# A transformer block's prelude: one modulation sum on VectorE, one on TensorE, and x normed in place

## The chip, the cores and the metric

The kernel runs on one core of a Trainium2 chip. TensorE multiplies matrices, VectorE and ScalarE work element by element, GpSimd does a few copies and subtractions, and SyncE (SP) issues nearly all transfers. The metric is device time in microseconds. Smaller is better.

## The reference, cut to what matters

One block for a sequence of 1024 tokens of width 1024 in float32: an adaptive modulation from a vector c, a token mixer of two branches (an attention with a forget gate and a recurrent one), and a convolutional feed-forward part. The prelude is its first lines:

```python
mod = jax.nn.silu(c) @ w_mod[l] + b_mod[l]
shift1, scale1, gate1, shift2, scale2, gate2 = jnp.split(mod, N_MOD, axis=-1)
u = modulate(rms_norm(h, ln1_g[l]), shift1, scale1)   # xn * (1 + scale) + shift
proj = u @ w_in
```

`w_mod` is 1024 x 6144. The prelude needs the two of its six segments that give shift1 and scale1, each 1024 x 1024 (eight tiles of 128 rows, 512 KB a tile). x is eight such tiles too. u is wanted with the model dimension on the partitions, so x is transposed on the way.

## The kernel before, in words

**Tiling.** Partitions are 128 wide. u is held as two tiles of 128 x 8 x 1024: `u_hi`, a copy rounded to the type fp32r, and `u_lo`, what the rounding left. A product with a weight is three matmul passes (hi x hi, hi x lo, lo x hi), and each weight tile `raw_in` is split in the same way by a ScalarE cast (`hi_in`) and a VectorE subtraction (`lo_in`).

**The prelude** (the block that opens the pools `st` and `stp`) has its own order on SP, VectorE, ScalarE and TensorE: written order.

- `load_x` issues the eight x tiles in two halves of four; each takes a slot of the tag `xt` (eight slots).
- `square` sums the squares of each x tile on ScalarE, and `norm_x` makes the reciprocal root for a half, `rstd`, and four scaled identity matrices `dg` from it.
- `warm(n)` issues n matmuls of 128 x 384 whose results nobody reads (tile `idle`).
- `turn` transposes a 128-column piece of a half by four matmuls against `dg`, so that norm and transpose are one; ScalarE copies the result from PSUM (two slots of tag `tp`) into `uf`. Sixteen turns, half 0 first. A float32 matmul is two instructions in the profile, so the 64 products are 128 records.
- `mod_load` issues the eight weight tiles of a segment: of scale first (four slots of tag `mw`), then of shift (slots of `xt` and `mw` by turns, as they come free).
- `mod_add` multiplies a weight tile with one element of silu(c) for each partition and adds it to `acc`, on VectorE; `mod_sum` then sums `acc` over the partitions with eight matmuls against a column of ones (tile `mps`). First scale is done (giving `A1`), then shift (giving `m1`), with warm matmuls between.
- Two weight tiles of `w_in` (`low_raw`: 24 and 25), `w2`, `g2` and the rest of the constants are loaded behind.
- `u_steps` makes u column by column: VectorE scales and shifts `uf` in place, ScalarE rounds it to `u_hi`, VectorE subtracts to `u_lo`. `low_part` follows each column with four matmuls (tile `low`), and with sixteen more when a half is complete. Between columns 3 and 4, and 5 and 6, of half 0 VectorE also splits the two `w_in` tiles.

**Behind the prelude**, `weave` mixes the products of the other `w_in` tiles (`rkv_items`: tile `ps_rkv`) with the decay chains. TensorE's order is written by the same walk in the program; those of the other engines come from a scheduler. `load_w` brings a `w_in` tile through one of two slots of tag `raw`, which `low_raw` and `w2` use too; the first of them is issued while u is still being made.

Of the kernel before, what the change touches and what calls it, by code (L numbers as in the profile page):

```python
# [9 lines left out]
F32 = mybir.dt.float32  # L10
F32R = mybir.dt.float32r
AF = mybir.ActivationFunctionType
ALU = mybir.AluOpType
# [118 lines left out]
def hybrid_block(ctx: ExitStack, tc: tile.TileContext, a, out):  # L132
# [122 lines left out]
    def load_w(src, name, pool=None, n=1024, scale=None, tags=("whi", "wlo"), bufs=2):  # L255
# [14 lines left out]
        else:  # L270
            nc.scalar.copy(hi, raw)  # L271
# [73 lines left out]
    with ExitStack() as es:  # L345
# [67 lines left out]
        with tc.tile_pool(name="st", bufs=1) as st, tc.tile_pool(name="stp", bufs=2, space=PS) as stp, \  # L413
# [17 lines left out]
            def norm_x(half):  # L431

                hs = slice(half * 4, half * 4 + 4)
                rms_rstd(rstd[:, hs], ssq[:, hs])
                for j in range(half * 4, half * 4 + 4):
                    ts(dg[:, j, :], ident, rstd[:, j : j + 1], None, op0=ALU.mult)

            def mod_load(i, tags):
                ws = [st.tile([128, D], F32, tag=tags[kt % len(tags)], name=f"wm{i}{kt}", bufs={"mw": 4, "xt": 8}[tags[kt % len(tags)]])
                      for kt in range(KT)]  # L440
                for kt, w in enumerate(ws):
                    nc.sync.dma_start(w, a["w_mod"][kt * 128 : kt * 128 + 128, i * D : i * D + D])
                return ws, st.tile([128, D], F32, name=f"acc{i}")
# [6 lines left out]
            def mod_add(kt, ws, acc):  # L450
                if kt == 0:
                    ts(acc, ws[kt], sc[:, 0:1], None, op0=ALU.mult)
                else:
                    stt(acc, ws[kt], sc[:, kt : kt + 1], acc, op0=ALU.mult, op1=ALU.add)

            def mod_sum(i, acc):
                for j0 in (0, 4):
                    ps = stp.tile([128, 4], F32, tag="mp", name=f"mps{i}{j0}")
                    for j in range(4):
                        c0 = (j0 + j) * 128  # L460
                        mm(ps[:, j : j + 1], acc[:, c0 : c0 + 128], ones[:, 0:1], start=True, stop=True)
                    tt(m1[:, i * 8 + j0 : i * 8 + j0 + 4], ps, V("b_mod", i * 8 + j0, 4), op=ALU.add)
                    if i == 1:
                        stt(A1[:, j0 : j0 + 4], m1[:, 8 + j0 : 12 + j0], 1.0, V("ln1_g", j0, 4), op0=ALU.add, op1=ALU.mult)

            def turn(kt, half, xs):
                ps = stp.tile([128, NH], F32, tag="tp", name=f"tr{half}_{kt}")
                for j in range(4):
                    mm(ps[:, j * 128 : j * 128 + 128], xs[j][:, kt * 128 : kt * 128 + 128], dg[:, half * 4 + j, :], start=True, stop=True)
                return ps  # L470

            def u_steps(half):

                cs = slice(half * NH, half * NH + NH)
                for kt in range(KT + 1):
                    if kt < KT:
                        x = uf[half][:, kt, :]
                        ts(x, x, A1[:, kt : kt + 1], m1[:, kt : kt + 1], op0=ALU.mult, op1=ALU.add)
                        nc.scalar.copy(u_hi[:, kt, cs], x)
# [30 lines left out]
            dg = xwa.rearrange("p (j s) -> p j s", s=128)  # L510
            idle = pb.tile([128, NH], F32, tag="big", name="idle")
            xs = [load_x(half) for half in range(2)]
            m = [mod_load(1, ("mw",)), None]
            uf = [st.tile([128, KT, NH], F32, name=f"uf{half}") for half in range(2)]
            warm(28)
# [3 lines left out]
            for half in range(2):  # L519
                for kt in range(KT):  # L520
                    nc.scalar.copy(uf[half][:, kt, :], turn(kt, half, xs[half]))
            m[1] = mod_load(0, ("xt", "mw"))
# [8 lines left out]
            for i in (1, 0):  # L531
                for kt in range(KT):
                    mod_add(kt, *m[1 - i])
                mod_sum(i, m[1 - i][1])
                warm((6, 40)[i])
# [1436 lines left out]
```

## Time and profile before

| | |
|---|---|
| median of 3 runs | 1701.49 us (1699.32 to 1701.51) |
| the profiled execution: its time | 1699.35 us |
| its span, first to last instruction | 1697.6 us |
| mean granted TensorE clock over the span | 0.991 |
| busy: TensorE, VectorE, ScalarE, GpSimd | 97%, 72%, 48%, 8% |
| first transpose of the prelude | 12.88 us |
| VectorE's first addition of a weight tile | 17.46 us |
| first column of u (VectorE, L478) | 47.16 us |
| first matmul behind the low products (`ps_rkv`) | 75.08 us |

All starts in the text are microseconds from the first instruction. Each engine works off its own queue in order; a busy share says how long it worked, not whether anyone waited for it. "PEclk" in the windows is the share of TensorE's full clock that was granted. The matmul records overlap, and their ends are modelled, so a rate is read from how many start in a stretch, not from the length of one.

### The profile page before, as it was taken

The numbers are of one execution on the slowest core, as the hardware profiler recorded it, in microseconds if no ns is written. First come the engines' busy times: TensorE is split into PE (matmuls) and PEld (weight loads), VectorE is DVE, ScalarE is ACT, GpSimd is POOL, SyncE is SP. The second block draws the span as 40 slices with busy tenths as digits, with TensorE's granted clock in tenths as the row PEclk, the third lists the DMA queues.
The fourth block names the chain that finished last, engine by engine and source line by source line (L and its number), as shares of the span: only waits on it lengthen the run. The fifth ranks groups of instructions, "written<-read, shape, count | busy, mean of one in ns | idle before, by whom it ended". The sixth has DMA issues, their size and how long they took to land.

```text
span 1697.6 us, 26285 instructions
## 1 busy us (share of the span) xinstructions
PE 1649.3 (97%) x9886; PEld 1351.7 (80%) x9886; DVE 1218.1 (72%) x2402; ACT 810.7 (48%) x1482; POOL 127.8 (8%) x151
## 2 busy tenths in 40 slices
PE   7999999999999998999989999999999999999998
PEld 7767877787877777888878888888888888888886
DVE  4776787778776624888767534897777777787677
ACT  5553334334354555766732223654444444454455
POOL 0010101111111001212022000000000000000000
PEclk9999999999999999999999999999999999999999
DMA  8487743533332226543177611133332233484463
GB/s 329 145 310 207 194 129 93 137 104 113 99 114 79 93 70 163 145 125 109 39 291 267 223 62 63 50 106 103 121 106 100 93 118 106 158 290 149 128 215 109
DMA packets 120975, 239.87 MB, mean 141 GB/s; under 512 B 39888, under 2 KB 48336, under 8 KB 120848
## 3 DMA queue, kind: packets, MB, share of 16 engines
q1 hardware_dynamic: 112896, 220.94, 39.5%
q0 software_dynamic: 7952, 17.25, 3.8%
q8 instruction: 78, 1.28, 0.3%
q14 instruction: 49, 0.40, 0.1%
HBM read 172.59 MB, written 65.54 MB: 140 GB/s over the span
## 4 chain that ended last, share of the span: by engine, by line
PE 82%; DVE 9%; DMA 4%; ACT 3%; issue 1%; SPq 1%; DVEq 0%; ACTq 0%
PE X L140 13%; PE D L140 12%; PE Y L140 6%; PE gt L140 6%; PE wo L140 5%; PE br L140 5%; PE ps_rkv L140 5%; PE qk L140 4%; PE W L140 3%; PE rk_ps L140 3%; PE v L140 2%; PE ov L140 2%; PE lg L140 2%; PE sp L140 2%; PE tr L140 2%; PE tp L144 2%
## 5 line engine op out<-in xcount | busy, mean ns | idle before, releaser
L140 PE MATMUL D<-op,op 128*128 128x512 f32 x924 | 209.8, 389 | 0.0
L140 PEld LDWEIGHTS D<-op,op 128*128 128x128 f32 x924 | 173.4, 188 | 36.3 <-DVE op L1235 0.3
L140 PE MATMUL X<-T_m,S 128*128 128x512 f32 x440 | 107.2, 390 | 0.2
L140 PEld LDWEIGHTS X<-T_m,S 128*128 128x128 f32 x440 | 82.5, 188 | 18.2 <-ACT x L1511 0.6
L1234 ACT CAST op<-g 128x512 fp32r<-128x512 f32 x77 | 47.8, 621 | 73.4 <-PE D L140 48.3
L1235 DVE TENSOR_TENSOR op<-g,op 128x512 fp32r<-128x512 f32 x77 | 53.0, 688 | 41.3 <-ACT op L1234 41.2
L1471 DVE SCALAR_TENSOR_TENSOR c<-ab,vec,c 128x512 f32<-128x512 f32 x88 | 65.9, 750 | 19.5 <-ACT c L1474 17.9
L779 DVE TENSOR_TENSOR t<-E,M 128x60 f32<-128x60 f32 (+24 forms) x248 | 57.2, 231 | 31.5 <-DMA M<-sm 26.2
L273 DVE TENSOR_TENSOR lo_in<-raw_in,hi_in 128x512 fp32r<-128x512 f32 x84 | 56.4, 706 | 30.0 <-PE gt L140 12.1
L1435 DVE TENSOR_TENSOR S<-ur,S 128x512 fp32r<-128x512 f32 x66 | 45.5, 691 | 35.4 <-ACT S L1431 35.2
L1431 ACT CAST S<-ur 128x512 fp32r<-128x512 f32 x66 | 41.0, 622 | 55.6 <-DVE ur L1424 30.6
L1435 DVE TENSOR_TENSOR A<-ur,A 128x512 fp32r<-128x512 f32 x64 | 44.0, 688 | 31.2 <-ACT A L1431 31.0
L271 ACT CAST hi_in<-raw_in 128x1024 fp32r<-128x1024 f32 x42 | 43.9, 1048 | 46.9 <-PE ps_rkv L140 16.9
L140 PE MATMUL Y<-T_h,A 128*128 128x512 f32 x264 | 63.4, 389 | 0.0
L140 PE MATMUL Y<-T_h,S 128*128 128x512 f32 x264 | 63.3, 389 | 0.0
L1051 ACT ACTIVATE P<-lg,nm 128x896 f32<-128x896 f32 (+3 forms) x64 | 47.5, 743 | 28.6 <-DVE nm L1047 19.6
L140 PE MATMUL X<-B_b,A 128*128 128x512 f32 x252 | 60.8, 390 | 0.0
L140 PE MATMUL W<-B_f,A 128*128 128x512 f32 x252 | 60.6, 389 | 0.0
L781 DVE TENSOR_TENSOR E<-E,t 128x60 f32<-128x60 f32 (+24 forms) x248 | 53.7, 216 | 5.8
L140 PEld LDWEIGHTS Y<-T_h,A 128*128 128x128 f32 x264 | 49.6, 188 | 10.3
L140 PEld LDWEIGHTS Y<-T_h,S 128*128 128x128 f32 x264 | 49.6, 188 | 10.3
L1431 ACT CAST A<-ur 128x512 fp32r<-128x512 f32 x64 | 39.9, 623 | 34.5 <-PE X L140 31.5
(469 smaller groups left out, 4163.9 us busy)
## 6 DMA issues: line engine op xcount, KB each, us to landing
raw_in<-in_w_in SPq DMA_DIRECT2D x50, 512.0 KB, 4.1
wm<-in_w_mod SPq DMA_DIRECT2D x48, 512.0 KB, 6.7
ur<-in_w_up SPq DMA_DIRECT2D x44, 512.0 KB, 4.1
g<-d_g SPq DMA_DIRECT2D x35, 512.0 KB, 3.7
d_g<-gs SPq DMA_DIRECT2D x44, 256.0 KB, 2.0
d_g<-c SPq DMA_DIRECT2D x33, 256.0 KB, 4.5
d_st<-qh SPq DMA_DIRECT2D x64, 128.0 KB, 2.5
d_gate<-gs SPq DMA_DIRECT2D x32, 256.0 KB, 3.0
```

Source lines behind the costliest of these rows:

```text
L140: nc.tensor.matmul(o, lhsT, rhs, start=start, stop=stop, skip_group_check=more)
L144: nc.tensor.transpose(o, i, eye)
L271: nc.scalar.copy(hi, raw)
L273: nc.vector.tensor_tensor(lo[:, c : c + NH], raw[:, c : c + NH], f32(hi[:, c : c + NH]), op=ALU.subtract)
L779: tt(tv, E32[:, 0:J, s : s + 1].to_broadcast([128, J, W]), M32[:, s : s + 1, s + 1 : 32].to_broadcast([128, J, W]), op=ALU.mult)
L781: tt(E32[:, 0:J, s + 1 : 32], E32[:, 0:J, s + 1 : 32], tv, op=ALU.add)
L1051: nc.scalar.activation(e[:, 0:n], lg[:, 0:n], AF.Exp, bias=nm[:, 0:1], accum_out=nm[:, 1:2])
L1234: nc.scalar.copy(hi, src)
L1235: tt(lo, src, f32(hi), op=ALU.subtract)
L1431: nc.scalar.copy(hi, src)
L1435: tt(lo, src, f32(hi), op=ALU.subtract)
L1471: stt(c, ab[:, x + hf * NH : x + hf * NH + NH], V("conv_w", 22 * x + i), c, op0=ALU.mult, op1=ALU.add)
```

## The change

Three parts.

**The sums.** The weight tiles of shift and scale are now loaded by turns (shift 0, scale 0, shift 1, ...) through one ring of five `mw` slots, each load issued when the tile five before it has been used. VectorE adds the shift tiles as before (`shift_add`). A scale tile is no longer added up on VectorE: `scale_add` multiplies its eight 128 x 128 pieces on TensorE with the 128 x 1 column of silu(c) and accumulates in the PSUM tile `scale`, which starts from `b_mod` (one product with the identity). `mod_sums` finishes in pieces of 1, 1, 2 and 4 columns: the column sums of `acc`, the last scale tile, and VectorE's two operations for each piece.

**The transposes.** `norm_x` multiplies the four x tiles of a half by `rstd` in place, 128 x 1024 each. `turn` then uses TensorE's transpose operation against the plain identity, one record for each 128 x 128 piece. The turns stand between the sums, two for each pair of weight tiles, and the halves alternate after every two.

**The columns of u.** Every second column is scaled and shifted by ScalarE instead of VectorE, and the first later cast of a `w_in` tile on ScalarE is told to stand behind the last rounding of u. The warm matmuls of 40 and 6 are gone, and the first 28 are 36.

TensorE's instructions from the last transposes to the first low product, before (`mps` are the column sums; x4 is four in a row):

```order
L140 MATMUL tr_7_313<-xwa,xt_154 128x128
L140 MATMUL mps_359<-cst,acc_172 128x1 x4
L140 MATMUL mps_366<-cst,acc_172 128x1 x4
L140 MATMUL idle<-cst 128x384 x40
L140 MATMUL mps_421<-cst,acc_335 128x1 x4
L140 MATMUL mps_427<-cst,acc_335 128x1 x4
L140 MATMUL idle<-cst 128x384 x6
L140 MATMUL low_441<-u_hi,hi_in_338 128x512
```

The same engine now, one round of the loop, the second scale tile's:

```order
L144 MATMUL tr_0_253<-cst,xt_153 128x128
L144 MATMUL tr_0_253<-cst,xt_155 128x128
L144 MATMUL tr_0_253<-cst,xt_157 128x128
L144 MATMUL tr_0_253<-cst,xt_159 128x128
L144 MATMUL tr_1_262<-cst,xt_153 128x128
L144 MATMUL tr_1_262<-cst,xt_155 128x128
L144 MATMUL tr_1_262<-cst,xt_157 128x128
L144 MATMUL tr_1_262<-cst,xt_159 128x128
L140 MATMUL scale<-sc,wm_167 128x1 x8
```

All transposes stood ahead of all sums; now eight transposes and eight one-column products alternate, seven times, and the eighth scale tile is left for the end. There the pieces wait for VectorE (in brackets the engine or queue whose semaphore is waited for):

```order
L140 MATMUL shift<-cst,acc 128x1 [waits DVE_49]
L140 MATMUL scale<-sc,wm_360 128x1 [waits DMAHW0_49]
L140 MATMUL shift<-cst,acc 128x1 [waits DVE_49]
L140 MATMUL scale<-sc,wm_360 128x1 [waits DVE_49]
L140 MATMUL shift<-cst,acc 128x1 [waits DVE_49]
L140 MATMUL scale<-sc,wm_360 128x1 [waits DVE_49]
L140 MATMUL shift<-cst,acc 128x1
L140 MATMUL scale<-sc,wm_360 128x1
L140 MATMUL shift<-cst,acc 128x1 [waits DVE_49]
L140 MATMUL scale<-sc,wm_360 128x1 [waits DVE_49]
```

Each new piece writes a PSUM tile that VectorE reads for the piece before, and waits for it. On ScalarE, at the second half of u, before (`hi_in_645` is the first `w_in` tile behind the low ones) and then now:

```order
L479 CAST u_hi<-uf_174 128x512 x2
L271 CAST hi_in_645<-raw_in_643 128x1024
L479 CAST u_hi<-uf_174 128x512 x6
L547 CAST w2h<-w_344 128x1024
L506 ACTIVATE sh_low_594<-low_441,vec 128x512
```

```order
L480 ACTIVATE uf_144<-uf_144,m_103,A_102 128x512
L483 CAST u_hi<-uf_144 128x512
L559 CAST w2h<-w_418 128x1024
L510 ACTIVATE sh_low_604<-low_451,vec 128x512
L271 CAST hi_in_655<-raw_in_653 128x1024
L271 CAST hi_in_662<-raw_in_660 128x1024
```

The cast of that tile went from between u's columns to behind them. TensorE's order behind the low products is the same in both.

The diff:

```diff
--- before.py
+++ after.py
@@ -268,7 +268,9 @@
             late_lo.append((hi, lo, raw))
             weave.spawn(lower(9000), 0)
         else:
-            nc.scalar.copy(hi, raw)
+            i = nc.scalar.copy(hi, raw)
+            if "u" in marks:
+                tc.add_manual_dep(i.ins, marks.pop("u").ins.name, NOSYNC)
             for c in range(0, n, NH):
                 nc.vector.tensor_tensor(lo[:, c : c + NH], raw[:, c : c + NH], f32(hi[:, c : c + NH]), op=ALU.subtract)
         return hi, lo
@@ -432,41 +434,40 @@
 
                 hs = slice(half * 4, half * 4 + 4)
                 rms_rstd(rstd[:, hs], ssq[:, hs])
-                for j in range(half * 4, half * 4 + 4):
-                    ts(dg[:, j, :], ident, rstd[:, j : j + 1], None, op0=ALU.mult)
-
-            def mod_load(i, tags):
-                ws = [st.tile([128, D], F32, tag=tags[kt % len(tags)], name=f"wm{i}{kt}", bufs={"mw": 4, "xt": 8}[tags[kt % len(tags)]])
-                      for kt in range(KT)]
-                for kt, w in enumerate(ws):
-                    nc.sync.dma_start(w, a["w_mod"][kt * 128 : kt * 128 + 128, i * D : i * D + D])
-                return ws, st.tile([128, D], F32, name=f"acc{i}")
+                for j in range(4):
+                    ts(xs[half][j], xs[half][j], rstd[:, half * 4 + j : half * 4 + j + 1], None, op0=ALU.mult)
+
+            def mod_load(kt, i, tag):
+                w = st.tile([128, D], F32, tag=tag, name=f"wm{i}{kt}", bufs={"mw": 5, "xt": 8}[tag])
+                nc.sync.dma_start(w, a["w_mod"][kt * 128 : kt * 128 + 128, i * D : i * D + D])
+                return w
 
             def warm(n):
 
                 for _ in range(n):
                     mm(idle[:, 0:NC1], cst[:, 0:128], cst, start=True, stop=True)
 
-            def mod_add(kt, ws, acc):
+            def shift_add(kt, w):
                 if kt == 0:
-                    ts(acc, ws[kt], sc[:, 0:1], None, op0=ALU.mult)
+                    ts(acc, w, sc[:, 0:1], None, op0=ALU.mult)
                 else:
-                    stt(acc, ws[kt], sc[:, kt : kt + 1], acc, op0=ALU.mult, op1=ALU.add)
-
-            def mod_sum(i, acc):
-                for j0 in (0, 4):
-                    ps = stp.tile([128, 4], F32, tag="mp", name=f"mps{i}{j0}")
-                    for j in range(4):
-                        c0 = (j0 + j) * 128
-                        mm(ps[:, j : j + 1], acc[:, c0 : c0 + 128], ones[:, 0:1], start=True, stop=True)
-                    tt(m1[:, i * 8 + j0 : i * 8 + j0 + 4], ps, V("b_mod", i * 8 + j0, 4), op=ALU.add)
-                    if i == 1:
-                        stt(A1[:, j0 : j0 + 4], m1[:, 8 + j0 : 12 + j0], 1.0, V("ln1_g", j0, 4), op0=ALU.add, op1=ALU.mult)
+                    stt(acc, w, sc[:, kt : kt + 1], acc, op0=ALU.mult, op1=ALU.add)
+
+            def scale_add(kt, w, j):
+                mm(scale[:, j : j + 1], w[:, j * 128 : j * 128 + 128], sc[:, kt : kt + 1], start=False, stop=kt == KT - 1, more=True)
+
+            def mod_sums(j0, j1, w):
+
+                for j in range(j0, j1):
+                    mm(shift[:, j : j + 1], acc[:, j * 128 : j * 128 + 128], ones[:, 0:1], start=True, stop=True)
+                    scale_add(KT - 1, w, j)
+                tt(m1[:, j0:j1], shift[:, j0:j1], V("b_mod", j0, j1 - j0), op=ALU.add)
+                stt(A1[:, j0:j1], scale[:, j0:j1], 1.0, V("ln1_g", j0, j1 - j0), op0=ALU.add, op1=ALU.mult)
 
             def turn(kt, half, xs):
                 ps = stp.tile([128, NH], F32, tag="tp", name=f"tr{half}_{kt}")
                 for j in range(4):
-                    mm(ps[:, j * 128 : j * 128 + 128], xs[j][:, kt * 128 : kt * 128 + 128], dg[:, half * 4 + j, :], start=True, stop=True)
+                    transpose(ps[:, j * 128 : j * 128 + 128], xs[j][:, kt * 128 : kt * 128 + 128], ident)
                 return ps
 
             def u_steps(half):
@@ -475,8 +476,11 @@
                 for kt in range(KT + 1):
                     if kt < KT:
                         x = uf[half][:, kt, :]
-                        ts(x, x, A1[:, kt : kt + 1], m1[:, kt : kt + 1], op0=ALU.mult, op1=ALU.add)
-                        nc.scalar.copy(u_hi[:, kt, cs], x)
+                        if kt % 2:
+                            nc.scalar.activation(x, x, AF.Identity, scale=A1[:, kt : kt + 1], bias=m1[:, kt : kt + 1])
+                        else:
+                            ts(x, x, A1[:, kt : kt + 1], m1[:, kt : kt + 1], op0=ALU.mult, op1=ALU.add)
+                        marks["u"] = nc.scalar.copy(u_hi[:, kt, cs], x)
                     if kt > 0:
                         k = kt - 1
                         tt(u_lo[:, k, cs], uf[half][:, k, :], f32(u_hi[:, k, cs]), op=ALU.subtract)
@@ -507,19 +511,30 @@
                     prev = sh[:, NH : NH + 1]
                     stt(dst[:, hf * NH : hf * NH + NH], low_ps[j][hf], omu[:, ti : ti + 1], sh[:, 0:NH], op0=ALU.mult, op1=ALU.add)
 
-            dg = xwa.rearrange("p (j s) -> p j s", s=128)
             idle = pb.tile([128, NH], F32, tag="big", name="idle")
+            acc = st.tile([128, D], F32, name="acc")
+            scale, shift = (stp.tile([128, 8], F32, tag="mp", name=x) for x in ("scale", "shift"))
+            uf = [st.tile([128, KT, NH], F32, name=f"uf{half}") for half in range(2)]
             xs = [load_x(half) for half in range(2)]
-            m = [mod_load(1, ("mw",)), None]
-            uf = [st.tile([128, KT, NH], F32, name=f"uf{half}") for half in range(2)]
-            warm(28)
+
+            mw = deque(mod_load(n // 2, n % 2, "mw") for n in range(5))
+            warm(36)
+            mm(scale, ident, V("b_mod", 8, 8), start=True, stop=False, more=True)
             for half in range(2):
                 square(half, xs[half], range(4))
                 norm_x(half)
-            for half in range(2):
-                for kt in range(KT):
-                    nc.scalar.copy(uf[half][:, kt, :], turn(kt, half, xs[half]))
-            m[1] = mod_load(0, ("xt", "mw"))
+            for n in range(2 * KT):
+                kt, i = divmod(n, 2)
+                w = mw.popleft()
+                k, half = kt // 2 * 2 + i, kt % 2
+                nc.scalar.copy(uf[half][:, k, :], turn(k, half, xs[half]))
+                if i == 0:
+                    shift_add(kt, w)
+                elif kt < KT - 1:
+                    for j in range(KT):
+                        scale_add(kt, w, j)
+                if n + 5 < 2 * KT:
+                    mw.append(mod_load((n + 5) // 2, (n + 5) % 2, "mw"))
             low_raw = [low_w(24, wp, ("whi", "wlo"), 2), low_w(25, st, ("xt", "xt"), 8)]
             low = [x[1:] for x in low_raw]
             w2 = rp.tile([128, S], F32, tag="raw", name="w2")
@@ -528,11 +543,8 @@
                     nc.sync.dma_start(w2[r * 64 : r * 64 + 64, j * 512 : j * 512 + 512], a["w2a2"][j * 64 : j * 64 + 64, :])
             nc.sync.dma_start(g2, a["g2"])
             nc.sync.dma_start(cst2, a["cst"][:, NC1:])
-            for i in (1, 0):
-                for kt in range(KT):
-                    mod_add(kt, *m[1 - i])
-                mod_sum(i, m[1 - i][1])
-                warm((6, 40)[i])
+            for j0, j1 in ((0, 1), (1, 2), (2, 4), (4, 8)):
+                mod_sums(j0, j1, w)
             for raw, hi, _ in low_raw:
                 nc.scalar.copy(hi, raw)
             low_ps = [[stp.tile([128, NH], F32, tag=("low", "tp")[hf], name=f"low{j}{hf}") for hf in range(2)] for j in range(2)]
```

## The prediction

> **What bounds the kernel now.** The page first: TensorE is busy nearly all the time, and the chain of waits runs mostly through it.
>
> ```profile
> PE 1649.3 (97%) x9886; PEld 1351.7 (80%) x9886; DVE 1218.1 (72%) x2402; ACT 810.7 (48%) x1482; POOL 127.8 (8%) x151
> PE 82%; DVE 9%; DMA 4%; ACT 3%; issue 1%; SPq 1%; DVEq 0%; ACTq 0%
> ```
>
> So a microsecond won or lost in the prelude reaches the end, since behind it stands a TensorE that hardly pauses. The shares say nothing of the prelude itself; the chain in order of time, cut to its first 75 us (start, length, what), does:
>
> ```profile
> 17.17 14.59 PE tr L140 x112
> 31.76 1.70 PE mps L140 x16
> 33.76 0.76 DVE acc L452
> 34.54 1.30 DVE acc L454
> ...
> 42.46 1.30 DVE acc L454
> 43.89 3.17 PE mps L140 x16
> 47.16 0.56 DVE uf L478
> ...
> 57.76 12.85 PE low L140 x51
> ```
>
> Two strands add up: TensorE's transposes until 31.8, then VectorE's second sum (33.8 to 43.9), then its column sums. The first column of u is formed at 47.16. That is the moment to move; the first `ps_rkv` matmul follows at 75.08, 27.9 us later.
>
> Next, the clock that TensorE was granted. The windows view (stretch, length, busy time of PE, PEld, DVE, ACT, POOL with counts, PEclk, DMA share, GB/s):
>
> ```profile
> 13.60:17.00 3.40, 1.23 (x11) 1.04 (x10) 0.33 (x2) 3.27 (x9) 0.00 (x0) 1.00 1.02 365
> 17.00:20.40 3.40, 3.23 (x15) 3.23 (x16) 3.33 (x6) 1.19 (x3) 0.00 (x0) 0.50 0.97 335
> 44.30:47.70 3.40, 3.40 (x17) 3.40 (x17) 0.78 (x4) 0.00 (x0) 0.00 (x0) 0.50 0.02 5
> 47.70:51.10 3.40, 3.40 (x10) 2.87 (x10) 3.17 (x7) 2.22 (x4) 0.00 (x0) 0.50 0.01 2
> 962.50:965.90 3.40, 3.40 (x30) 3.27 (x28) 0.25 (x2) 0.00 (x0) 0.00 (x0) 1.00 0.88 361
> 965.90:969.30 3.40, 3.40 (x14) 3.01 (x14) 0.33 (x2) 0.00 (x0) 0.00 (x0) 0.50 0.02 7
> ```
>
> The clock is whole or half, in steps of 3.4 us. A stretch with 1.23 us of work in 3.40 (36%) is followed by one at half clock. The last two rows matter most: from 962.5 to 965.9 TensorE is never idle, and yet the next stretch is at 0.50. What it did there, with the same kind of instruction at whole and at half clock, and transposes at half clock (start, length, instruction):
>
> ```profile
> 963.17 4.32 PE L140 MATMUL mps<-cst,acc 128*128 128x1 f32 x32
> 31.60 1.84 PE L140 MATMUL mps<-cst,acc 128*128 128x1 f32 x16
> 44.22 2.83 PE L140 MATMUL mps<-cst,acc 128*128 128x1 f32 x13
> 712.03 1.05 PE L144 MATMUL tp<-cst,P 128*128 128x128 f32 x4
> 712.74 0.67 PE L140 MATMUL ov<-th,vh 128*128 128x256 f32 x2
> ```
>
> It was matmuls of one column against a 128x128 weight: they fill TensorE's time but do not hold its clock. 44.30 to 47.70 says the same from the other side: packed with them, begun at half clock, and still at half clock after it. A one-column record costs 1.84/16 = 0.115 us at whole clock and 2.83/13 = 0.218 at half.
>
> **The change part by part.**
>
> *The scale sum goes to TensorE.* Eight VectorE additions leave (0.75 + 7 x 1.3, about 10 us, the chain's 33.8 to 43.9). In their place stand 64 one-column matmuls, eight for each weight tile. A mod_sum of eight was 16 records (31.60), so each is two: 16 records a tile. The two trailing sums of 16 records become one tail, mod_sums, of 32. The warm matmuls of 6 and 40 go; 28 become 36.
>
> *Norm and transposes.* Scaling the identity (0.87 us a half) becomes scaling x in place, four 128x1024 VectorE operations a half. The nearest row is the first addition, started 17.46 with the next at 18.25: 0.79 each.
>
> ```profile
> 11.53 0.87 DVE L436 TENSOR_SCALAR xwa<-cst,rstd 128x128 f32<-128x128 f32 x4 [8.19 <-ACT rstd L298]
> 16.68 0.87 DVE L436 TENSOR_SCALAR xwa<-cst,rstd 128x128 f32<-128x128 f32 x4 [4.28 <-ACT rstd L298]
> 17.46 0.75 DVE L452 TENSOR_SCALAR acc<-wm,sc 128x1024 f32<-128x1024 f32 x1
> 12.88 1.95 PE L140 MATMUL tr<-xwa,xt 128*128 128x128 f32 x16
> 33.30 7.18 PE L140 MATMUL idle<-cst 128*128 128x384 f32 x40
> ```
>
> Half 0 is normed at 11.53 + 3.16 = 14.7, half 1 at 16.68 + 3.16 = 19.8. The warm matmuls, which ended at 12.88, now end 8 x 0.18 later, at 14.3; that hides the norm of half 0. Half 1's is not hidden, and the shift additions queue behind it on VectorE: the first moves from 17.46 to 19.8. The 128 transpose records become 64. Their cost: 0.115 at whole clock as the records they replace (1.95/16 = 0.12); at half clock between 0.18 (four from 712.03 to 712.74) and 0.215 (3.23/15 in the stretch from 17.0). I take 0.20, between two near ends.
>
> *What the clock does.* One round of the new loop is eight transposes and 16 one-column records: at whole clock 8 x 0.115 + 16 x 0.115 = 2.76 us. Only the 0.92 us of transposes can count, 33%, less than the 36% that lost the clock at 17.0, and with bursts some stretch sees less. At half clock a round has 1.60 us of transposes in 5.09, at most 47% of a stretch of 3.4. The stretch 965.90 to 969.30 ran wide matmuls from 967.4 on, some 55%, and stayed at half. So I expect half clock from some point between 16.6 and 20.4 (the warm matmuls end at 14.3; the steps are not tied to the program), say 18.7, until the wide matmuls of the low products have filled a step.
>
> Here two sentences of the Trainium skill pull apart. TensorE: Matmul & The Clock Gate, section "HAM oscillation — how this bites in real kernels", asks only that TensorE have no idle gaps over some 3.4 us; by that this loop would keep the clock (the first rival), but the row from 962.5 has no gap and differs. Its "Part 4: PE-mode transpose" says that transposes do not count as busy; no stretch of this trace has them alone, and by that the share is near 0 and not 33%.
>
> *The sum.* When the second weight tile lands, from the rate:
>
> ```profile
> 0.00:10.00 10.00, 4.02 (x13) 4.02 (x14) 0.65 (x9) 6.45 (x10) 0.92 (x5) 1.00 0.82 292
> 10.00:20.00 10.00, 7.66 (x46) 7.47 (x46) 4.13 (x11) 7.97 (x17) 0.00 (x0) 0.85 1.02 379
> 32.59 0.16 DVE L462 TENSOR_TENSOR m<-mps,vec 128x4 f32<-128x4 f32 x1 [3.24 <-PE mps L140]
> 32.78 0.16 DVE L464 SCALAR_TENSOR_TENSOR A<-m,vec 128x4 f32<-128x4 f32 x1
> ```
>
> x, constants and two tiles are 5.54 MB, 2.92 of them by 10.0: landed at 10 + 2.62/0.379 = 16.9. Scale sum 0 then runs from 17.0 to 19.0, the last records slowly. The transposes of half 1 wait for its norm and end at 20.9. Scale sum 1: 16 x 0.218 = 3.5, to 24.4. Five more rounds of 5.09: 49.8. The last eight transposes: 51.4. The tail: 32 x 0.218 = 7.0, to 58.4. It is cut into 1, 1, 2 and 4 columns, and each piece waits for VectorE's two operations (0.16 each) on the piece before: about 0.3 hidden badly, 0.6 behind the last. First column of u: 59.3, against 47.16: **+12.1 us**. SP issues a tile when the slot five back is free; with TensorE this slow that is always early, so the transfers are hidden. Were TensorE fast, they would be the next to be late (a rival).
>
> *The columns of u.*
>
> ```profile
> 49.01 0.54 DVE L478 TENSOR_SCALAR uf<-uf,A,m 128x512 f32<-128x512 f32 x1
> 49.46 0.68 DVE L482 TENSOR_TENSOR u_lo<-uf,u_hi 128x512 fp32r<-128x512 f32 x1
> 50.06 0.54 DVE L478 TENSOR_SCALAR uf<-uf,A,m 128x512 f32<-128x512 f32 x1
> 62.39 1.05 ACT L271 CAST hi_in<-raw_in 128x1024 fp32r<-128x1024 f32 x1 [2.27 <-DMA raw_in<-in_w_in]
> 63.18 0.39 PE L140 MATMUL low<-u_hi,hi_in 128*128 128x512 f32 x1
> 71.39 3.85 PE L140 MATMUL low<-u_hi,lo_in 128*128 128x512 f32 x16
> ```
>
> Two columns cost VectorE 2 x 1.05; with every second one scaled on ScalarE 0.46 + 2 x 0.60 = 1.66, while ScalarE does three operations of some 0.55. Half 0 loses 4 x 0.44 = 1.8 on VectorE, but TensorE at half clock becomes the longer strand there, so some 1.2 of it stays. The cast of a w_in tile that stood among u's casts and waited 2.27 us for its transfer now comes after the last: TensorE's 8.21 us from 63.18 to 71.39 fall to 32 x 0.23 = 7.4. Together **-2.0** (from -3 to -1). The second w_in tile now takes the slot that w2 leaves, after GpSimd's subtraction; TensorE needs it only 5.4 us after the low products, and u's end lies earlier before their end than it did: nothing, and up to +2 if VectorE's queue behind it slips.
>
> Sum: +10.1. The profiled execution had 1699.35 for a span of 1697.6; that gives 1709.5. It was the fastest of the runs shown, 2.1 below their median, two of which stand at 1701.5; by the median it is 1711.6. I say **1711**.
>
> **The rivals.**
>
> *The clock holds.* One mechanism, on the other side: one-column matmuls count enough beside the transposes. For it: the stretch 962.5 had 20% of wide work, so a small weight per record is not excluded; against it: both sides of the gate in the rows above. Rounds of 2.76: from 20.6, 22.4, five rounds to 36.2, transposes 37.1, tail 3.7 + 0.6 + 0.6, u at 42.0: -5.2, with the low products -7.2: 1694. It decides where fewer than some 45% of the 180 records after 20 us run at half clock: u may start at 49.2 before the gain of 2.0 is eaten, 28.2 us for 180 records, 0.157 each between 0.115 and 0.21.
>
> *The clock holds, but the transfers set the pace.* The ring of four slots gave a tile per 1.90 us:
>
> ```profile
> 22.35 1.28 DVE L454 SCALAR_TENSOR_TENSOR acc<-wm,sc,acc 128x1024 f32<-128x1024 f32 x1 [0.17 <-DMA wm<-in_w_mod]
> ...
> 28.06 1.28 DVE L454 SCALAR_TENSOR_TENSOR acc<-wm,sc,acc 128x1024 f32<-128x1024 f32 x1 [0.39 <-DMA wm<-in_w_mod]
> ```
>
> Now five slots hold both halves' tiles: 1.52 to 1.90 a tile. The first reused slot is free at 20.6, lands 4.1 later, ten more follow: 40.0 to 43.8; with the tail u at 44.9 to 48.7, in all -4.3 to -0.5, middle 1699. Against it: the stretch to 20.0 shows 379 GB/s, 1.4 us a tile.
>
> *Half clock in part only*, because the transposes win a step back: between the two, near 1702.
>
> **How the numbers follow.** Half clock throughout 0.86; clock holds 0.08; transfers 0.04; in part 0.02. Runs of this kernel differ by 0.13%; 0.2% (3.4 us) is what can be told. Slower: the first, 0.86. Same: half of the transfers' case and the partial one, 0.04. Faster: 0.10. The likeliest case's own range is 1705 to 1716: the step's place 0.8 either way, transposes at 0.18 or 0.215 (-1.1, +0.8), tail +2, u -1 to +1, behind it +2, and 2 for which run it is measured against. The range 1702 to 1717 takes in the partial case and leaves out the fast ones.
>
> **What would show it.** The windows after: PEclk 0.50 from about 19 to 60; scale sums of 3.5 us and not 1.8; VectorE's additions waiting for tiles or for nothing, far ahead of TensorE; the first column of u near 59; `ps_rkv` near 85. PEclk 1.00 between 21 and 40 with u near 42 proves me wrong at the step on the clock. If the clock is half and u starts before 55, a record's price is wrong; if u starts near 59 and the end moves by less than 8, the low products or what stands behind them gave it back.

## The result, and the profile after

The changed kernel takes **1710.69 us** (median of five runs, 1709.02 to 1714.02) beside 1701.48 for the kernel before (five runs, 1699.32 to 1701.51): a ratio of 1.006, 95% interval 1.0046 to 1.0074. It is slower by 0.6%. The prediction said 1711, range 1702 to 1717, with 0.86 on slower. The profiled execution after took 1711.48 for a span of 1709.70, against 1699.35 and 1697.6 before.

Busy time of the engines, and the clock in 40 slices, on the page of the changed kernel:

```profile
PE 1666.4 (97%) x9898; PEld 1368.3 (80%) x9898; DVE 1210.5 (71%) x2388; ACT 815.3 (48%) x1490; POOL 127.3 (7%) x151
PEclk7799999999999999999999999999999999999999
```

TensorE has 12 instructions more and 17.1 us more busy time, so the same kind of work must run slower somewhere. The first two slices (85 us) stand at 7, that is, some 70% of the clock. The windows view (columns as in the prediction) shows where:

```profile
17.00:20.40 3.40, 3.02 (x21) 3.02 (x22) 3.36 (x6) 0.57 (x2) 0.00 (x0) 0.80 0.94 375
19.00:51.10 32.10, 32.10 (x155) 32.10 (x156) 10.04 (x9) 7.58 (x13) 0.00 (x0) 0.50 0.65 228
51.10:58.10 7.00, 6.89 (x34) 6.80 (x32) 1.19 (x8) 2.51 (x4) 0.00 (x0) 0.50 0.00 1
```

The clock halves at about 19.0 (0.80 over the stretch from 17.0: 2.0 us whole, 1.4 at half) and stays at half through the loop, in which TensorE has not one idle moment (32.10 of 32.10), and through the tail. It came back at 63.4, when the wide low products had run for a while: 44.4 us at half clock in one piece. Before, the prelude had two short pieces, 3.4 and 6.8 us.

The chain of waits after, in order of time (start, length, what):

```profile
17.38 2.10 PE scale L140 x16
19.48 1.81 PE tr L144 x8
21.29 3.20 PE scale L140 x16
...
49.56 1.81 PE tr L144 x8
...
58.11 0.56 DVE uf L482
58.69 0.62 ACT u_hi L483
59.31 0.73 ACT uf L480
60.05 1.14 ACT u_hi L483 x2
```

Where before the chain had transposes and then VectorE's sum, it now has TensorE alone: rounds of 3.20 + 1.81 = 5.01 us, seven sums of 16 records and the transposes between them. The first column of u is formed at 58.11, 10.9 us later than before. VectorE, which held the chain for 10 us before, now waits: the waits view from 17 to 60 us (who waited for whom: total, times, longest):

```profile
DVE acc L454 <- DMA wm<-in_w_mod: 13.6, 5, 3.9
```

VectorE's additions wait 13.6 us for weight tiles. Most of these loads are issued when an earlier addition has freed a slot: by the waits of SP's queue, its loads of weight tiles waited 10.8 us for VectorE's additions, 10.3 for other tiles to land and only 1.4 for TensorE's sums. VectorE's waits cost nothing: the last addition ended at 42.7, the tail needs its result at 51.2.

### The profile page after: what moved, and what is told of

It reads as the page before. It is cut to its first block, busy times and chain, and to the rows that moved or that the text cites. A ratio compares the mean times of both kernels' runs of the same rounds, so it can differ in the third digit from the quotient of the medians.

```text
span 1709.7 us, 26288 instructions
## 1 busy us (share of the span) xinstructions
PE 1666.4 (97%) x9898; PEld 1368.3 (80%) x9898; DVE 1210.5 (71%) x2388; ACT 815.3 (48%) x1490; POOL 127.3 (7%) x151
## 4 chain that ended last, share of the span: by engine, by line
PE 80%; DVE 9%; DMA 5%; ACT 3%; issue 1%; SPq 1%; POOL 0%; DVEq 0%; ACTq 0%
PE X L140 13%; PE D L140 12%; PE Y L140 6%; PE gt L140 5%; PE wo L140 5%; PE br L140 5%; PE ps_rkv L140 5%; PE W L140 3%; PE qk L140 3%; PE rk_ps L140 3%; PE lg L140 2%; PE ov L140 2%; PE sp L140 2%; PE tp L144 2%; PE scale L140 1%; PE v L140 1%
## 5 line engine op out<-in xcount | busy, mean ns | idle before, releaser
L275 DVE TENSOR_TENSOR lo_in<-raw_in,hi_in 128x512 fp32r<-128x512 f32 x84 | 57.5, 719 | 30.4 <-PE gt L140 12.1
L1447 DVE TENSOR_TENSOR S<-ur,S 128x512 fp32r<-128x512 f32 x66 | 45.5, 691 | 35.6 <-ACT S L1443 35.5
L140 PEld LDWEIGHTS Y<-T_h,A 128*128 128x128 f32 x264 | 49.6, 188 | 10.4
L140 PEld LDWEIGHTS Y<-T_h,S 128*128 128x128 f32 x264 | 49.5, 188 | 10.3
```

What stands on the lines that cost most here:

```text
L140: nc.tensor.matmul(o, lhsT, rhs, start=start, stop=stop, skip_group_check=more)
L275: nc.vector.tensor_tensor(lo[:, c : c + NH], raw[:, c : c + NH], f32(hi[:, c : c + NH]), op=ALU.subtract)
L1447: tt(lo, src, f32(hi), op=ALU.subtract)
```

## The experiments

Each is compared with the kernel before on the same chip. "u" stands for the start of the first column of u in the profiled execution: 47.2 before, 58.1 after.

The theory: one-column matmuls do not hold TensorE's clock, the 64 new ones fill the prelude with them, and at half clock each costs about twice. The rivals: the transposes or one-column matmuls are simply too many and slow at any clock; transposes are what fails to hold the clock; the transfers set the pace.

### Wide matmuls put between: e1_wide

```
     nc.scalar.copy(uf[half][:, k, :], turn(k, half, xs[half]))
+    warm(4)
```

> The changed kernel with four wide matmuls (128x384, result unread) behind each turn, so eight more a round. Theory, the clock gate: the wide matmuls raise the counted share of a round from 33% to about 55% (0.92 of transposes and 1.44 of wide matmuls in 4.20 us), PEclk stays near 1.00, a scale sum takes 1.8 us, u begins near 52 and the time falls by about 5 us against the change, to 1704-1707, although TensorE has 64 instructions more. If transposes do not count, the share is only 34% and the clock stays half. Rival, TensorE is simply bound by the number of its instructions: a round grows by 8 x 0.32, u begins near 76, 1728 us.

1705.23 us (five runs, 1704.41 to 1707.63), ratio 1.0035 (1.0022 to 1.0048); u at 50.8. The windows view of this kernel, then its timeline for TensorE (start, length, instruction, count):

```profile
17.40:45.80 28.40, 28.40 (x227) 28.15 (x226) 11.63 (x11) 8.48 (x15) 0.00 (x0) 1.00 0.79 282
```

```profile
23.43 0.64 PE L144 MATMUL tr<-cst,xt 128*128 128x128 f32 x4
23.82 0.95 PE L140 MATMUL idle<-cst 128*128 128x384 f32 x4
...
25.75 1.84 PE L140 MATMUL scale<-sc,wm 128*128 128x1 f32 x16
```

Matmuls whose product nobody reads were added (eight of 128x384 a round), and u came 7.3 us earlier than in the changed kernel. The clock is 1.00, the scale sum takes 1.84 and not 3.41 for its 16 records, the round 4.02 and not 5.01 although it holds eight wide matmuls more. So the clock is the cause of most of the loss, and the transfers would have kept up with rounds of 4.02. The first rival fell: at whole clock the same work, wide matmuls included, has u 3.6 us behind the kernel before and not 10.9, and the first `ps_rkv` matmul (77.06) 2.0 behind and not 9.35. The other 3.9 us by which this execution's span is longer (1703.5 against 1697.6) arise behind the prelude (see "The sum" below). Of a round, transposes and wide matmuls are 25.75 - 23.43 = 2.3 us, 58%.

### Half as many: e8_wide2

```
+    warm(2)
```

> As the run with eight wide matmuls a round, with four. Theory: 0.92 of transposes and 0.72 of wide matmuls in 3.48 us is 47%, above what held the clock elsewhere (50%) or just below it; if it holds, u begins near 46 and the time is 1699-1701; if not, a round takes 6.4, u begins near 67 and the time is near 1719. Between the two where the clock is lost in some of the runs only.

1704.04 us (ten runs, 1697.84 to 1711.89), ratio 1.0032 (1.0013 to 1.0051). The profiled execution held the clock and had u at 46.8:

```profile
17.40:42.00 24.60, 23.39 (x194) 22.44 (x194) 11.73 (x12) 7.87 (x14) 0.00 (x0) 1.00 0.84 293
```

The runs divide by the mean granted clock of each: 1697.84, 1698.38, 1698.97 and 1699.87 at 0.990 to 0.992; 1703.77 to 1708.30 at 0.987; 1710.14 and 1711.89 at 0.983 to 0.984. The changed kernel itself lies at 0.978 to 0.980 in all its runs, the one with eight wide matmuls at 0.988 to 0.991. TensorE's timeline gives the share:

```profile
26.61 0.64 PE L144 MATMUL tr<-cst,xt 128*128 128x128 f32 x4
...
28.23 1.84 PE L140 MATMUL scale<-sc,wm 128*128 128x1 f32 x16
29.93 0.63 PE L144 MATMUL tr<-cst,xt 128*128 128x128 f32 x4
```

Transposes and wide matmuls are 28.23 - 26.61 = 1.62 us of a round of 3.32, 49%: the edge at which, by the mean clocks, it is kept in one run and lost in the next. For the other runs only the mean clock is known, not where it was lost.

### Transposes as products with the identity: e2_two_pass

```
-    transpose(ps[...], xs[j][...], ident)
+    mm(ps[...], xs[j][...], ident, start=True, stop=True)
```

> The changed kernel with its transposes again as two-record matmuls, now against the plain identity (x stays normed in place). Theory: matmuls of 128 columns count, 1.84 us of 3.68 in a round is 50%, the clock holds, u begins near 48 and the time is about that of the kernel before, 1699-1703. Rival, instruction count: 64 records more at 0.21 each, u near 71, 1724 us.

1706.45 us (ten runs, 1698.96 to 1729.8), ratio 1.005 (1.0014 to 1.0085), which leaves out the run of 1729.8 (the other nine have a median of 1703.27); u at 49.6. Windows and TensorE's timeline:

```profile
20.40:23.80 3.40, 3.40 (x22) 3.40 (x20) 2.33 (x2) 1.17 (x2) 0.00 (x0) 0.59 0.75 241
23.80:27.20 3.40, 3.40 (x33) 3.40 (x32) 0.76 (x1) 1.17 (x2) 0.00 (x0) 1.00 0.95 337
```

```profile
24.47 2.03 PE L140 MATMUL tr<-cst,xt 128*128 128x128 f32 x16
26.34 1.84 PE L140 MATMUL scale<-sc,wm 128*128 128x1 f32 x16
```

With twice the transpose records the profiled execution won the clock back after one step and kept it until 47.1; its rounds take 3.57. The median missed its expectation because the runs divide again: 1698.96 to 1703.27 at clocks of 0.988 to 0.992, two near 1709.8 at 0.984 to 0.985, and 1723.49 to 1729.8 at 0.974 to 0.977, where the doubled transposes are paid at half clock. The transposes are 26.34 - 24.47 = 1.87 of a round of 3.57, 52%. What looked in the change like a saving, one pass for two, took away half of the records that can keep the clock here.

### All transposes first: e4_turns_first

```
+for half in range(2):
+    for k in range(KT):
+        nc.scalar.copy(uf[half][:, k, :], turn(k, half, xs[half]))
 for n in range(2 * KT):
     ...
-    k, half = kt // 2 * 2 + i, kt % 2
-    nc.scalar.copy(uf[half][:, k, :], turn(k, half, xs[half]))
```

> The changed kernel with all sixteen turns ahead of the first sum, so that transposes stand alone on TensorE from about 15 to 25 us and one-column matmuls alone after it. If transposes hold the clock: PEclk 1.00 until at least 24, and half from then on. If they do not (the rule of the Trainium skill, TensorE: Matmul & The Clock Gate, Part 4): PEclk 0.50 by 22, while TensorE is still at transposes. Either way 112 records of a scale sum run at half clock and u begins at 52-57, 1704-1710 us.

1705.37 us (six runs, 1700.71 to 1708.02), ratio 1.0025 (1.001 to 1.0039); u at 54.1. This parts the two kinds of instruction in time. Windows, then timeline:

```profile
19.00:22.40 3.40, 2.99 (x22) 2.10 (x20) 3.33 (x4) 2.63 (x5) 0.00 (x0) 1.00 0.66 214
22.40:25.80 3.40, 2.89 (x21) 2.18 (x22) 0.38 (x1) 2.76 (x6) 0.00 (x0) 1.00 0.91 327
25.80:29.20 3.40, 3.40 (x33) 3.40 (x32) 1.28 (x1) 1.09 (x2) 0.00 (x0) 1.00 0.42 131
29.20:32.60 3.40, 3.40 (x19) 3.40 (x18) 1.28 (x1) 0.00 (x0) 0.00 (x0) 0.54 0.90 314
```

```profile
25.22 1.16 PE L144 MATMUL tr<-cst,xt 128*128 128x128 f32 x8 [0.18 <-ACT uf L528]
26.21 20.93 PE L140 MATMUL scale<-sc,wm 128*128 128x1 f32 x112
```

From 19.0 to 25.8 TensorE does transposes alone, with gaps, and the clock is whole. From 26.2 on it does one-column matmuls alone, without a gap (3.40 of 3.40), and after one step, near 29.5, the clock is half, until the wide work 30 us later. So it is the one-column matmuls that lose the clock and not the transposes. Both kinds load a weight of 128 columns for each record (the second count of a row); what sets them apart is that 128 columns stream past it or one.

### The scale summed on VectorE again: e3_scale_on_dve

```
-mm(scale[:, j : j + 1], w[:, ...], sc[:, kt : kt + 1], ...)
+stt(acc2, w, sc[:, kt : kt + 1], acc2, op0=ALU.mult, op1=ALU.add)
...
```

> The changed kernel with the scale sum back on VectorE (a second accumulator; the ring has four slots, since the second accumulator takes the room of the fifth); order of loads, in-place norm, transposes and columns of u stay. Theory: the loss is the 112 one-column records at half clock; without them VectorE's 16 additions or the ring set the pace, 39 to 47, the tail of 32 records at half clock follows, u begins at 46-52 and the time is 1699-1705. Rival, the loss is in the norm in place or the transposes: u stays at 56 or later, 1709 or more.

1703.22 us (ten runs, 1699.88 to 1704.19), ratio 1.001 (0.9996 to 1.0024); u at 50.5. The timeline of TensorE, then of VectorE; the bracket is the idle time before and what ended it:

```profile
20.25 8.73 PE L144 MATMUL tr<-cst,xt 128*128 128x128 f32 x48 [0.24 <-ACT uf L534]
41.06 0.59 PE L140 MATMUL shift<-cst,acc 128*128 128x1 f32 x2 [12.08 <-DVE acc L454]
```

```profile
42.51 1.28 DVE L460 SCALAR_TENSOR_TENSOR acc<-wm,sc,acc 128x1024 f32<-128x1024 f32 x1 [1.51 <-DMA wm<-in_w_mod]
```

The other parts of the change are all in this kernel, the scale sum on TensorE is undone (and with it the ring's fifth slot), and the interval no longer shows a loss. The additions now end at 43.8, held by the transfers, and an idle TensorE (12.08 us) begins its tail at half clock. With this sum on VectorE too, the transfers and that tail bring u to within 3.4 us of where the kernel before has it.

### The columns of u alone: e5_u_only

Into the kernel before went only the part at u: every second column is scaled on ScalarE, and the cast of a w_in tile comes behind u.

```
-ts(x, x, A1[:, kt : kt + 1], m1[:, kt : kt + 1], op0=ALU.mult, op1=ALU.add)
+if kt % 2:
+    nc.scalar.activation(x, x, AF.Identity, scale=A1[:, kt : kt + 1], bias=m1[:, kt : kt + 1])
+else:
+    ts(x, x, A1[:, kt : kt + 1], m1[:, kt : kt + 1], op0=ALU.mult, op1=ALU.add)
...
```

> The kernel before with the third part of the change alone: every second column of u on ScalarE, and the first later cast of a w_in tile behind the last rounding of u. Theory: the first column of u stays at 47.2, the way from it to the first ps_rkv falls from 27.9 to 26.3 us as in the changed kernel, the time by 1 to 2 us to 1698-1699. Rival: the tile's later cast holds up what stands behind the low products by as much, and the time is that of before.

1696.86 us (twelve runs, 1694.3 to 1700.83), ratio 0.9988 (0.9977 to 1.0000). The way from u to the first `ps_rkv` matmul is 26.3 us, against 27.9 before and 26.3 after the whole change: this edit brings 1.6, and it is the good one of the change. The column of u itself also starts earlier, at 45.2 and not 47.2 as expected: in this execution the last sums began 0.7 us earlier (43.17) and fell on a whole clock (1.92 us for 16 records, 3.17 before). The interval of the time reaches 1.0000, so the gain in time is not clear of the noise.

### The operands exchanged: e7_moving

The same sums, but the column of c is the 128x1 weight and the weight tile streams through, 512 columns at a time. The result is a row, which ScalarE copies to SBUF, and eight matmuls with one row turn it into columns.

```
-for j in range(KT):
-    mm(scale[:, j : j + 1], w[:, j * 128 : j * 128 + 128], sc[:, kt : kt + 1], ...)
+for hf in range(2):
+    mm(srow[hf][0:1, :], sc[:, kt : kt + 1], w[:, hf * NH : hf * NH + NH], ...)
...
```

> The changed kernel with the operands of the scale products exchanged: the column of silu(c) is the weight (one column) and the 128x512 half of a weight tile streams past it, four records a tile; the row of sums is copied by ScalarE and turned into columns by eight small products at the end. Theory, what streams counts: a tile's records are 512 columns wide, a round of 2.6 us is nearly all counted, PEclk stays 1.00, the transfers or VectorE set the pace, u begins at 42-46 and the time is 1694-1698. Rival, a weight of one column does not count: half clock, a round of 5.0 us, u near 58, 1709.

1700.27 us (twelve runs, 1698.12 to 1701.76), ratio 1.0004 (0.9994 to 1.0015); u at 48.1. Windows and TensorE's timeline:

```profile
17.40:42.00 24.60, 21.93 (x89) 8.10 (x89) 11.68 (x12) 8.30 (x16) 0.00 (x0) 1.00 0.87 322
42.00:48.10 6.10, 6.00 (x32) 5.60 (x32) 1.15 (x8) 2.47 (x3) 0.00 (x0) 0.79 0.01 3
```

```profile
34.44 1.88 PE L140 MATMUL srow<-wm,sc 128*1 128x512 f32 x4 [1.45 <-DMA wm<-in_w_mod]
```

A tile costs 1.88 in four records, what sixteen one-column records cost at whole clock (1.84), and the clock holds without any wide matmul added. With that the loss is gone; u still missed 42 to 46, and the time 1694 to 1698. TensorE now waits for tiles (1.45 us at 34.44), which is the prediction's rival of the transfers, and the tail of one-column records took 6.2 us (41.9 to 48.05), from 45.5 on at half clock.

### Another way to shorten VectorE's strand: e6_defer and e9_defer_warm

The kernel before with the part at u; VectorE's two small operations on the scale sums are moved behind the shift additions, so that it does not wait for TensorE between its two sums; the eight columns of a sum lie in one tile; the six warm matmuls go.

```
-    mod_sum(i, m[1 - i][1])
-    warm((6, 40)[i])
+    sums.append(mod_sum(i, m[1 - i][1]))
+    warm((0, 40)[i])
...
+mod_use(1, sums[0])
+mod_use(0, sums[1])
```

> The kernel before with the third part, and with VectorE's operations on the scale column sums moved behind its additions for shift (both segments still summed on VectorE; the sums of eight columns in one PSUM tile; the six warm matmuls gone). Theory: VectorE's idle 4.4 us between the two segments (29.3 to 33.8) goes, the additions end near 39.5, the column sums run at whole clock behind 40 warm matmuls, u begins at 42-43.5 and the time is 1693-1695, below both kernels. Rival, the transfers of the shift tiles set the pace there: u at 46 or later, 1698-1699.

1695.32 us (twelve runs, 1692.66 to 1697.97), ratio 0.9976 (0.9964 to 0.9988); u at 44.7. TensorE's timeline:

```profile
40.85 3.57 PE L140 MATMUL mps<-cst,acc 128*128 128x1 f32 x16 [2.05 <-DVE acc L456]
```

The shift additions end at 40.8 and not at 43.7 (39.5 was expected, with u at 42 to 43.5 and 1693 to 1695 us), but the last sum's 16 records take 3.57: the warm matmuls had ended 2.05 us before, and a step at half clock fell upon them. So the last run has 56 warm matmuls and not 40:

```
-    warm((0, 40)[i])
+    warm((0, 56)[i])
```

> The run with the deferred operations, with 56 warm matmuls instead of 40 ahead of the shift column sums, so that TensorE has no idle time there (it had 2.05 us, and the clock was half from 40.8 to 51.0). Theory: the warm matmuls end at 31.6 + 56 x 0.18 = 41.6, 0.8 later than the additions, but the sums of 16 records take 1.9 and not 3.6 us and the first low products run at whole clock: u begins near 43.8, 0.9 earlier, and the time falls by 1 us or a little more, to about 1694. Rival: what is late there is the additions alone, and the later start of the sums costs as much as the clock gives: 1695-1696.

**1693.09 us** (six runs, 1692.24 to 1694.81), ratio 0.9963 (0.995 to 0.9977): faster than both kernels of this case. TensorE's timeline:

```profile
33.25 9.98 PE L140 MATMUL idle<-cst 128*128 128x384 f32 x56
43.07 1.84 PE L140 MATMUL mps<-cst,acc 128*128 128x1 f32 x16
```

The sum is back at 1.84, as expected. But u came at 45.2, not 43.8, in the profiled execution: a step at half clock from 17.3 to 20.8 had delayed the transposes, and the warm matmuls, begun behind them, ended only at 43.2. The 2.2 us between the medians of these two kernels, which ran on different chips, is thus not shown to come from an earlier u.

## Why the prediction was right

**The clock.** Predicted: half from about 18.7 until the wide low products have filled a step. Measured: 19.0 to 63.4. Its reading of the two gates in the profile before, that one-column matmuls fill TensorE's time but not its clock, is what the runs with the two kinds apart (26.2 to 29.5) and with the operands exchanged show. The rival "clock holds" needed one-column matmuls to count enough beside the transposes; PEclk 0.50 over the 32.1 us of the loop says that they do not. The sentence of the Trainium skill that the prediction set against the row (TensorE: Matmul & The Clock Gate, section "HAM oscillation — how this bites in real kernels": no idle gaps over some 3.4 us) is not enough for these records, since TensorE had no gap at all in those 32.1 us.

**The round.** Predicted 5.09 (1.60 for eight transposes, 3.49 for 16 records), measured 5.01 (1.81 and 3.20). Two errors went against each other: a transpose record costs 0.226 and not 0.20 at half clock, a one-column record 0.200 and not 0.218. The quoted 2.83 for 13 records held the modelled tail of the last one once: where 16 follow each other, as in the group from 21.29, the chain says 3.20.

**The start.** The first scale sum at 17.4 (17.0), the shift additions from 19.3 (19.8). VectorE's scaling of x in place costs (19.30 - 16.64)/4 = 0.67 us each and not 0.79, by the timeline:

```profile
16.64 2.74 DVE L438 TENSOR_SCALAR xt<-xt,rstd 128x1024 f32<-128x1024 f32 x4 [2.41 <-ACT rstd L300]
19.30 0.75 DVE L452 TENSOR_SCALAR acc<-wm,sc 128x1024 f32<-128x1024 f32 x1
```

**The tail.** The last transposes end at 51.4 as predicted. The tail takes 6.8, from the start of its first record to the end of its last, where 7.0 was predicted. Its first and last pieces on TensorE, and VectorE's answer:

```profile
51.16 0.42 PE L140 MATMUL shift<-cst,acc 128*128 128x1 f32 x2
...
57.42 0.56 PE L140 MATMUL scale<-sc,wm 128*128 128x1 f32 x2
```

```profile
58.02 0.16 DVE L465 SCALAR_TENSOR_TENSOR A<-scale,vec 128x4 f32<-128x4 f32 x1 [0.26 <-PE scale L140]
58.11 0.55 DVE L482 TENSOR_SCALAR uf<-uf,A,m 128x512 f32<-128x512 f32 x1
```

The hand-offs between its four cuts, for which 0.3 was added, show no gap: at half clock there is time for VectorE's two operations between them. The 0.6 behind the last sum was 0.1. Together u came at 58.1 and not at 59.3: +10.9 where +12.1 was predicted.

**The columns of u: the term that was mis-sized.** Predicted -2.0, measured 27.9 to 26.3, -1.6, in the changed kernel and in the run of this part alone. The 0.8 forecast for the second half came: its 32 low records took 7.41 us (73.29 to 80.70), 8.21 before. The miss lies in the first half, from the first column of u to the first of those records: 16.02 us before (47.16 to 63.18), 15.18 now (58.11 to 73.29), -0.84 and not -1.2. The step that failed there is "ScalarE does three operations of some 0.55". ScalarE's timeline in the changed kernel:

```profile
59.21 0.81 ACT L480 ACTIVATE uf<-uf,m,A 128x512 f32<-128x512 f32 x1
60.05 1.14 ACT L483 CAST u_hi<-uf 128x512 fp32r<-128x512 f32 x2
61.10 0.81 ACT L480 ACTIVATE uf<-uf,m,A 128x512 f32<-128x512 f32 x1
```

The operation with a scale and a bias costs 0.81, and a pair of columns 61.10 - 59.21 = 1.89 on ScalarE, more than the 1.66 that VectorE was to need. So ScalarE sets the pace of the first four columns, and the chain after shows it: its rows alternate between ACT uf and ACT u_hi. Two pairs with 0.23 us too much each are the size of the miss. From 62.6 to 68.9 VectorE, which also splits the two w_in tiles there, is the longer strand again. In the second half ScalarE sets the pace once more, but it costs nothing, since the low products run without a gap. This is read from the trace; no run tried another split.

**Behind the low products.** `ps_rkv` starts at 84.42 (about 85 was to be), 9.35 later than before. "Nothing, and up to +2" for the second w_in tile turned out small but not nothing. The chain there:

```profile
80.34 4.79 DMA raw_in<-in_w_in
85.21 1.06 ACT hi_in L271
...
86.90 0.68 DVE lo_in L275
...
95.76 0.67 DVE k L370
96.47 3.24 PE ps_rkv L140 x13
```

The tile's load was issued only when GpSimd's subtraction on w2 had ended, at 80.3; its cast starts at 85.21 and VectorE's part at 86.90, and VectorE's queue behind it runs late: the `ps_rkv` matmul at 96.47 waits 0.98 us for VectorE (`k`), where the same one before, at 86.72, waits 0.60. From there the changed kernel is 9.75 behind and not 9.35.

**The sum.** The medians differ by 9.2, near the 9.35 at `ps_rkv`. The forecast of 1711 was 0.3 above what came, and that close it is by luck: the start of u was put 1.2 too late, the gain at u's columns 0.4 too high, and the two profiled executions differ by 12.1, since from 170 us to 350 the changed kernel fell behind by some 3.5 us more. About 1 us of that is a wait of TensorE for VectorE (0.79 us at 181.95, none before). About 1 arises near 240 us, where the changed kernel has two steps at half clock (240.9 to 247.7) and the kernel before has one (232.1 to 235.5). The rest, 1.5, lies in the step from 312.6 to 316.0, half in the changed kernel and whole at the same work before. About 1 comes back later, in a step at half clock that only the kernel before has (709.9 to 713.3). Four of the matmuls in the step from 312.6, first in the changed kernel, then in the kernel before:

```profile
313.78 2.07 PE L140 MATMUL qk<-u_hi,lo_in 128*128 128x512 f32 x4
```

```profile
301.44 1.21 PE L140 MATMUL qk<-u_hi,lo_in 128*128 128x512 f32 x4
```

Over all the kernels run here the time from `ps_rkv` to the end lies between 1620.8 and 1626.4 (1622.5 before, 1625.3 after), although TensorE's order there is the same. Steps at half clock fall at other places in each trace and are part of it. Leaving out the last 20 us, the five traces with 17 us at half clock behind the prelude take 1620.8 to 1623.5, and the four with 24 to 27 us take 1624.1 to 1625.9; but the two with 20 us take 1621.0 and 1626.4, so they are not all of it. Why the steps fall where they do stays open.

## What to carry to other kernels

Idle time on TensorE is not free to be filled with any work: a matmul with one column against a 128x128 weight occupies the engine for two records of some 0.11 us and does not hold its clock, and at half clock it and the transposes around it cost nearly twice. Where a sum over rows is wanted from TensorE, put the vector in as the weight and let the wide matrix stream. And before replacing a two-pass transpose by a one-pass one beside such matmuls, ask in the windows of the profile what holds the clock there.

## What the runs showed of the hardware

**Transposes hold the clock, and win it back.** The prediction left open whether they count at all. In the run with all of them first, TensorE did nothing but transposes for 2.99 and 2.89 of 3.40 us, and the clock stayed at 1.00 until one-column matmuls had run alone for 3.3 us. The run with the scale summed on VectorE shows the other half. Its 48 transposes from 20.25 on are all that TensorE did from 20.8 to 24.2, at half clock, and the next step is whole:

```profile
20.80:24.20 3.40, 3.40 (x17) 2.80 (x16) 2.44 (x3) 2.28 (x4) 0.00 (x0) 0.50 0.95 313
24.20:27.60 3.40, 3.20 (x22) 2.10 (x20) 2.57 (x3) 2.88 (x6) 0.00 (x0) 1.00 1.02 360
```

The Trainium skill (TensorE: Matmul & The Clock Gate, "Part 4: PE-mode transpose") says that the full clock does not engage for them, since they do not count as busy in the same way; here the measurement decides against it.

**The edge is not sharp.** Where the transposes are 1.81 of 5.01 us, 36% (the changed kernel), the mean clock was low in every run; with 58% (eight wide matmuls) it was high in every run, and in the profiled one held until the tail. With 49 and 52% the runs of one and the same kernel went from 1697.84 to 1711.89 and from 1698.96 to 1729.8, in step with their mean clock. A kernel so near the edge has no time of its own, and a median over few runs of it says little.

**It is the streaming that counts, as far as these runs go.** Sixteen one-column records and four 512-column records take the same 1.84 to 1.88 us for the same weight tile. The first lose the clock; the second, whose weight has a single column, hold it, and so do transposes, with 128 columns. No run tests a width between 1 and 128.
